# Routing of an expert-choice layer on one core: two token chunks sorted at once, a threshold from two lists, 512-column output products, and dummy products on TensorE

## The chip, the cores and the metric

The kernel runs on 1 core of one Trainium2 chip. The metric is the device time of one execution in microseconds (us), given as the median of several runs. About 0.3% (3 us) is what a measurement of this kernel can tell from no change.

## What is computed

One encoder layer on 512 tokens of width 1024: three token mixers (neighbourhood attention, grouped-query attention, cross-attention into 256 memory tokens), each gated and projected, and then the part in which the change lies:

```
mix    = merged @ w_out
x      = layer_norm(alpha * x + mix)
logits = x @ w_router                      # 512 tokens x 16 experts
aff    = softmax(logits, axis=experts)
gate, idx = top_k(aff.T, 64)               # each expert takes its 64 best tokens
xs     = x[idx]
h      = xs @ w_gate_up[e];  ye = (silu(hg) * hu) @ w_down[e] * gate
x      = layer_norm(alpha * x + scatter_add(ye))
```

All inputs are float32. The weights of the 16 experts are 192 MB (12 MB each), the rest of the weights about 37 MB.

## The kernel before, in words

Everything is in one function with a schedule written out by hand: each engine (TensorE, VectorE, ScalarE, GpSimd) and each DMA queue works through its instructions strictly in program order, and a tile that is used again waits for its last reader. Tokens lie in four chunks `m` = 0 to 3 of 128.

**Weights of the mixers.** They come as 74 units of 128 x 1024 (512 KB), loaded by the SP queue two ahead into two "raw" tiles. ScalarE casts each to a high part (L84) and VectorE subtracts to get a low part (L85); a product is then three products, high x high, high x low and low x high, in a fast float32 format. The last 8 units are `w_out`. A unit's parts sit in rotating tiles, so unit i can be split only when unit i-3 is used up.

**Output products (L964 to L985 and `w_half`, L991).** `merged` lies transposed in `mh` and `ml` (high and low part). For the first 512 columns, two passes of 256 columns run over all four chunks; each pass takes two units (one for each half of the 1024-long inner dimension), and its four accumulators lie in the PSUM tags S, S, T, T for the first pass and mm, mm, mm, Y for the second. Then the other 512 columns are done chunk by chunk in halves of 256 columns (`w_half`, with 24 products each). `wo_evac` (L910) adds alpha x to each accumulator and takes statistics of 256 columns at a time on VectorE.

**Routing of a chunk.** `r_transpose` (L892) transposes the unnormed sum on TensorE and ScalarE copies it; `r_logits` (L901) multiplies it with the router's weights (which already hold the norm's gain, centred), in two halves that VectorE adds. `route` (L916) works out the row scale 1/sqrt(var) by three Newton steps on 128 x 1 columns, scales the logits, and makes the softmax (exponential on ScalarE). `r_back` (L946) transposes the 128 x 16 result to 16 x 128, and ScalarE copies it into `affA` or `affB`. `x1_norm` (L953) makes the normed rows: two small GpSimd steps, a scale and a cast of 128 x 1024 on ScalarE (L957, L959), and a subtraction on GpSimd (L960); the gather needs these.

**The sort (`rounds`, L996).** Each expert's threshold is its 64th best value. One round finds the 8 best of a row (MAX8) and replaces them by -1 (MATCH_REPLACE8); eight rounds give 64. A chunk's 64 best are put beside the next chunk and both are sorted again: chunk 0 (128 columns), chunk 1 with the best of 0, and, behind everything (L1069), chunks 2 and 3 with the best so far (264 to 320 columns). The sorts of chunks 0 and 1 are mixed with the steps of `route`. 16 partitions (one per expert) are in use. The steps of `w_half` and of routing follow each other as L1014 to L1064 have them.

**Threshold and gather.** The 64th value of each expert (L1071) is spread to all partitions by a product (`thp`, L1073), VectorE compares, `cnp` counts places by products with a triangle matrix (`tri_t`), `onehot` (L1095) builds 0/1 matrices and `gather` (L1105) picks the rows by products: 8 pieces for each group of four experts. For the first expert three pieces are made, and then pieces and gate/up products (`gate_up`, L1140, the products of L1149) alternate.

**Expert weights (`Ring`, L715).** They are loaded as 192 MB in pieces of 1 MB into 20 places that other tiles leave free, in a fixed order, issued by the SP queue. Places 7 to 10 (raw tiles among them) come free while w_out is split; 11 to 16 hold `mh`, the last split unit, `ml` and the low parts until the output products are done; 17 and 18 hold x until `x1_norm` is done; 19 holds the triangle matrix until the counts are done. Loads 20 and on wait until `gate_up` has used up a place (`done`, L770).

Of the kernel before, what the change touches and what calls it, by code (L numbers as in the profile page):

```python
# [40 lines left out]
def layer_kernel(ctx: ExitStack, tc: tile.TileContext, xt, xn, memt, wu, bgate, rpb, gains, wrt,  # L41
# [838 lines left out]
    def x1(m):  # L880
        return X1[m // 2][:, m % 2]
# [5 lines left out]
    affA = R("t", [NEXP, P + 192], "affA", bufs=2)  # L887
    affB = R("t", [NEXP, 320], "affB", bufs=2)

    XT, LG, MV, RS = {}, {}, {}, {}  # L890

    def r_transpose(m, k0, n, eng="act"):  # L892
# [6 lines left out]
        (nc.scalar.copy if eng == "act" else nc.vector.tensor_copy)(t, tp)  # L899

    def r_logits(m, h):  # L901
        lg = PB("mm", f"lg{m}{h}")
        for k in range(4 * h, 4 * h + 4):
            nc.tensor.matmul(lg[:, :NEXP], XT.pop((m, k)), wg_t[:, k], start=(k == 4 * h), stop=(k == 4 * h + 3))
        if h:
            LG[m] = lg
        else:
            nc.scalar.copy(lgA[:, m], lg[:, :NEXP])

    def wo_evac(m, acc, c0, n):  # L910
        c = slice(c0, c0 + n)
        nc.vector.scalar_tensor_tensor(x1(m)[:, c], x1(m)[:, c], DN_ALPHA, acc[:, :n], op0=ALU.mult, op1=ALU.add)
        for q in range(c0 // 256, (c0 + n) // 256):
            nc.vector.bn_stats(st_all[:, m, q], x1(m)[:, q * 256:(q + 1) * 256])

    def route(m):  # L916
        mv = small([P, 2], "lnmv")
        MV[m] = mv
        nc.vector.bn_aggr(mv, st_all[:, m])
        yield  # L920
        v, hv, y, a = (small([P, 1], n) for n in ("rv_v", "rv_h", "rv_y", "rv_a"))
        nc.vector.tensor_scalar(v, mv[:, 1:2], LN_EPS, None, op0=ALU.add)
        yield
        nc.vector.tensor_scalar(y.bitcast(I32), v.bitcast(I32), -0.5, RSQRT_SEED, op0=ALU.mult, op1=ALU.add)
        nc.vector.tensor_scalar(hv, v, -0.5, None, op0=ALU.mult)
        yield
        for i in range(3):
            nc.vector.tensor_scalar(a, y, hv, y, op0=ALU.mult, op1=ALU.mult)
            if i == 2:
                nc.vector.tensor_tensor(lgA[:, m], lgA[:, m], LG.pop(m)[:, :NEXP], op=ALU.add)  # L930
            yield
            nc.vector.tensor_scalar(y, a, 1.5, y, op0=ALU.add, op1=ALU.mult)
            yield
        RS[m] = y
        nc.vector.scalar_tensor_tensor(lgA[:, m], lgA[:, m], y, rb, op0=ALU.mult, op1=ALU.add)
        yield
        nm, sm, rc = (small([P, 1], n) for n in ("rnm", "rsm", "rrc"))
        nc.vector.tensor_reduce(nm, lgA[:, m], axis=AX.X, op=ALU.max, negate=True)
        ex = small([P, NEXP], "rex")
        nc.scalar.activation(ex, lgA[:, m], AF.Exp, bias=nm, accum_out=sm)  # L940
        yield
        nc.vector.reciprocal(rc, sm)
        yield
        nc.vector.tensor_scalar(aff[:, m], ex, rc, None, op0=ALU.mult)

    def r_back(m):  # L946
        ap = PB("Y", f"ap{m}")
        nc.tensor.transpose(ap[:NEXP, :P], aff[:, m], ident)
        c = (0, P + 64, 64, 64 + P)[m]
        dst = (affA if m < 2 else affB)[:, c:c + P]  # L950
        nc.scalar.copy(dst, ap[:NEXP, :P])

    def x1_norm(m):  # L953
        nb, r = (small([P, 1], n) for n in ("lnnb", "lnr13"))
        nc.gpsimd.tensor_scalar(r, RS[m], X_SCALE, None, op0=ALU.mult)
        nc.gpsimd.tensor_scalar(nb, MV[m][:, 0:1], r, -1.0, op0=ALU.mult, op1=ALU.mult)
        nc.scalar.activation(x1(m), x1(m), AF.Identity, bias=nb, scale=r)  # L957
# [6 lines left out]
    for q in range(2):  # L964
        banks = ("mm", "mm", "mm", "Y") if q == 1 else ("S", "S", "T", "T")
        accs = [PB(banks[m], f"wo{q}{m}") for m in range(NT)]
        for hf in range(2):
            u, = ws.take()
            h = u[0].rearrange("p (k c) -> p k c", k=4)
            lo = u[1].rearrange("p (k c) -> p k c", k=4)  # L970
            ws.prefetch(2)
            for m in range(NT):
                tok = slice(m * P, (m + 1) * P)
                acc = accs[m][:, :256]
                for k in range(4):
                    kk = 4 * hf + k
                    nc.tensor.matmul(acc, mh[:, kk, tok], h[:, k], start=(kk == 0), stop=False)
                    nc.tensor.matmul(acc, mh[:, kk, tok], lo[:, k], start=False, stop=False)
                    nc.tensor.matmul(acc, ml[:, kk, tok], h[:, k], start=False, stop=(kk == KD - 1))  # L979
                if hf == 1:  # L980
                    wo_evac(m, accs[m], q * 256, 256)
                    if q == 1 and m:
                        r_transpose(m - 1, 0, 4)
                    if q == 1 and m > 1:
                        r_logits(m - 2, 0)  # L985
    us = [ws.take(2)]
    ws.prefetch(2)
    us.append(ws.take(2))
    ring.upto(N_EARLY + 2)

    def w_half(m, j, hooks={}):  # L991
        acc = PB("S", f"woc{m}{j}")
        n_chunk(acc[:, :256], us[j], mh, ml, m, hooks)
        wo_evac(m, acc, 512 + j * 256, 256)

    def rounds(src, lead, dst):  # L996
        for r in range(8):
            win = src[:, lead - 8 * (r + 1) if lead else 0:]
            t = dst[:, 56 - 8 * r:64 - 8 * r]
# [14 lines left out]
    w_half(0, 0)  # L1014
    r_transpose(3, 0, 4)
    r_logits(2, 0)
    w_half(0, 1)
    r_logits(3, 0)
    r_transpose(0, 4, 2)
    w_half(1, 0)  # L1020
    r_transpose(0, 6, 2)
    r_logits(0, 1)
    all_of(route(0))
    w_half(1, 1)
    r_transpose(1, 4, 2)
    r_back(0)
    x1_norm(0)
    seg = rounds(affA[:, 0:P], 0, affA[:, P:P + 64])
    c1 = route(1)
    for _ in range(5):  # L1030
        steps(c1, seg)
    w_half(2, 0, {2: lambda: r_transpose(1, 6, 2)})
    r_logits(1, 1)
    for _ in range(8):
        steps(c1, seg)
    all_of(c1)
    all_of(seg)
    w_half(2, 1)
    r_transpose(2, 4, 2)
    r_back(1)  # L1040
    x1_norm(1)
    seg = rounds(affA[:, P:], 64, affB[:, 0:64])
    c2 = route(2)
    for _ in range(5):
        steps(c2, seg)
    w_half(3, 0, {2: lambda: r_transpose(2, 6, 2)})
    r_logits(2, 1)
    for _ in range(8):
        steps(c2, seg)
    all_of(c2)  # L1050
    x1_norm(2)
    w_half(3, 1)
    r_transpose(3, 4, 2)
    r_transpose(3, 6, 2)
    r_back(2)
    r_logits(3, 1)
    c3 = route(3)
    for _ in range(8):
        steps(c3, seg)
    all_of(c3)  # L1060
    all_of(seg)
    r_back(3)
    x1_norm(3)
    ring.upto(len(RING))  # L1064
# [3 lines left out]
    top = cp.tile([NEXP, 64], F32, name="top")  # L1068
    all_of(rounds(affB, 64, top))  # L1069
# [521 lines left out]
```

## Time and profile before

| | us |
|---|---|
| runs shown | 998.05, 998.72, 1001.01 |
| median | 998.72 |
| the profiled execution | 997.83 |
| its span, first to last instruction | 995.9 |
| TensorE busy | 955.8 (96%) |
| VectorE busy | 459.5 (46%) |
| ScalarE busy | 273.8 (27%) |
| GpSimd busy | 75.2 (8%) |
| mean granted clock of TensorE | 0.988 |

A profile line by group reads: source line, engine, operation, written tile, read tiles, shapes, count, then busy time, mean duration of one in ns, and the idle time of the engine ahead of it with what ended it. A line in order of time reads: start, duration, engine, line, operation, shapes, count, and in brackets the idle time ahead. SPq is the SP engine's DMA queue. A line of the table by stretch reads: from:to, length, busy time (and count) of PE, PEld (weight loads of TensorE), DVE, ACT and POOL, then the granted clock, the DMA engines' share and their GB/s. A busy TensorE is not one at its peak, since ends of products are modelled. TensorE's products of float32 are recorded as two.

### The profile page before, as it was taken

The numbers are of one execution on the slowest core, as the hardware profiler recorded it, in microseconds if no ns is written. First come the engines' busy times: TensorE is split into PE (matmuls) and PEld (weight loads), VectorE is DVE, ScalarE is ACT, GpSimd is POOL, SyncE is SP. The second block draws the span as 40 slices with busy tenths as digits, with TensorE's granted clock in tenths as the row PEclk, the third lists the DMA queues.
The fourth block names the chain that finished last, engine by engine and source line by source line (L and its number), as shares of the span: only waits on it lengthen the run. The fifth ranks groups of instructions, "written<-read, shape, count | busy, mean of one in ns | idle before, by whom it ended". The sixth has DMA issues, their size and how long they took to land.

```text
span 995.9 us, 13692 instructions
## 1 busy us (share of the span) xinstructions
PE 955.8 (96%) x5504; PEld 631.3 (63%) x5504; DVE 459.5 (46%) x897; ACT 273.8 (27%) x547; POOL 75.2 (8%) x77
## 2 busy tenths in 40 slices
PE   7999899999999999999968999999999999998998
PEld 7899787889888888889954334533353333432355
DVE  5437678664376566256582155331322222231327
ACT  5434345444354444333341010200020001100021
POOL 0002403000131231000040000000000000000002
PEclk9999999999999999999987999999999999999999
DMA  8221211111432332665448999999999999999992
GB/s 340 98 85 65 64 64 43 64 48 61 110 113 81 93 88 94 237 253 222 159 180 339 368 424 420 423 421 422 425 423 422 424 424 424 423 422 421 425 397 97
DMA packets 67422, 251.61 MB, mean 253 GB/s; under 512 B 14720, under 2 KB 19488, under 8 KB 54944
## 3 DMA queue, kind: packets, MB, share of 16 engines
q1 hardware_dynamic: 66784, 249.44, 64.1%
q10 hardware_dynamic: 576, 1.31, 0.3%
q8 instruction: 43, 0.70, 0.3%
q14 instruction: 19, 0.16, 0.0%
HBM read 247.84 MB, written 2.10 MB: 251 GB/s over the span
## 4 chain that ended last, share of the span: by engine, by line
PE 80%; DMA 9%; DVE 6%; ACT 2%; POOL 2%; issue 1%; SPq 0%; POOLq 0%; ACTq 0%
PE g L1149 10%; PE u L1149 9%; PE y L1182 8%; DMA gu<-in_wgu 5%; PE gate L231 4%; PE gate L233 4%; PE gate L232 4%; DMA dn<-in_wdn 3%; PE pr L231 2%; PE ga L1113 2%; PE pr L232 2%; PE pr L233 2%; PE cb L1249 2%; PE ga L1115 2%; PE nqk L233 1%; PE nqk L232 1%
## 5 line engine op out<-in xcount | busy, mean ns | idle before, releaser
L1149 PE MATMUL g<-gu,xs 128*64 128x512 f32 x512 | 134.6, 604 | 5.5 <-DMA gu<-in_wgu 5.4
L85 DVE TENSOR_TENSOR wlo<-raw,whi 128x1024 fp32r<-128x1024 f32 (+2 forms) x75 | 92.7, 1237 | 87.7 <-ACT whi L84 87.3
L1149 PE MATMUL u<-gu,xs 128*64 128x512 f32 x512 | 131.6, 592 | 0.2 <-DMA gu<-in_wgu 0.2
L1182 PE MATMUL y<-dn,hT 128*64 128x512 f32 x480 | 106.8, 594 | 2.4 <-DMA dn<-in_wdn 2.2
L84 ACT CAST yh<-y 64x512 fp32r<-64x512 f32 x30 | 17.4, 579 | 249.0 <-PE y L1182 221.1
L84 ACT CAST whi<-raw 128x1024 fp32r<-128x1024 f32 (+2 forms) x75 | 77.0, 1027 | 25.3 <-PE wo L979 9.4
L1149 PEld LDWEIGHTS u<-gu,xs 128*64 128x64 f32 x512 | 36.7, 137 | 73.6 <-issue 68.3
L85 DVE TENSOR_TENSOR yl<-y,yh 64x512 fp32r<-64x512 f32 x30 | 20.7, 689 | 135.7 <-ACT yh L84 125.1
L1182 PEld LDWEIGHTS y<-dn,hT 128*64 128x64 f32 x480 | 33.8, 137 | 72.1 <-issue 63.1
L1149 PEld LDWEIGHTS g<-gu,xs 128*64 128x64 f32 x512 | 31.3, 136 | 62.4 <-issue 43.9
L1252 DVE TENSOR_TENSOR acc<-acc,cb 128x512 f32<-128x512 f32 x56 | 35.4, 683 | 35.1 <-PE cb L1250 35.1
L1170 DVE COPY hT<-ht 128x512 f32<-128x512 f32 x16 | 11.0, 690 | 62.1 <-PE ht L1167 62.1
L1314 POOL TENSOR_TENSOR acc<-acc,ln2g 128x512 f32<-128x512 f32 x4 | 5.1, 1277 | 452.3 <-DVE l2s L1326 452.1
L231 PE MATMUL gate<-xha,whi 128*128 128x512 f32 x96 | 38.9, 406 | 0.0
L232 PE MATMUL gate<-xla,whi 128*128 128x512 f32 x96 | 37.5, 390 | 0.0
L233 PE MATMUL gate<-xha,wlo 128*128 128x512 f32 x96 | 37.5, 390 | 0.0
L233 PE MATMUL gate<-xhb,wlo 128*128 128x512 f32 x96 | 37.4, 389 | 0.0
L231 PE MATMUL gate<-xhb,whi 128*128 128x512 f32 x96 | 37.3, 389 | 0.0
L232 PE MATMUL gate<-xlb,whi 128*128 128x512 f32 x96 | 37.3, 389 | 0.0
L550 ACT ACTIVATE gp<-gs,nm 128x512 f32<-128x512 f32 x32 | 21.7, 683 | 52.3 <-DVE nm L549 52.3
L1159 ACT ACTIVATE tg<-g 128x512 f32<-128x512 f32 x16 | 9.6, 597 | 89.5 <-PE g L1149 89.5
L1160 DVE SCALAR_TENSOR_TENSOR tg<-tg,g 128x512 f32<-128x512 f32 x16 | 11.0, 685 | 38.7 <-ACT tg L1159 38.7
(382 smaller groups left out, 1990.3 us busy)
## 6 DMA issues: line engine op xcount, KB each, us to landing
gu<-in_wgu SPq DMA_DIRECT2D x95, 1024.0 KB
dn<-in_wdn SPq DMA_DIRECT2D x49, 1024.0 KB
raw<-in_wu SPq DMA_DIRECT2D x73, 512.0 KB
gu<-in_wgu SPq DMA_DIRECT2D x66, 512.0 KB
dn<-in_wdn SPq DMA_DIRECT2D x30, 512.0 KB
xr<-in_xt SPq DMA_DIRECT2D x4, 512.0 KB
x<-in_xn SPq DMA_DIRECT2D x2, 1024.0 KB
bf<-in_rpb SPq DMA_DIRECT2D x64, 24.0 KB
```

The source lines that it names most:

```text
L84: nc.scalar.copy(hi, src)
L85: nc.vector.tensor_tensor(lo, src, hi.bitcast(F32), op=ALU.subtract)
L231: nc.tensor.matmul(acc, w_h, rh[:, k], start=(k == 0), stop=False)
L232: nc.tensor.matmul(acc, w_h, rl[:, k], start=False, stop=False)
L233: nc.tensor.matmul(acc, w_l, rh[:, k], start=False, stop=(k == nk - 1))
L550: nc.scalar.activation(self.p[:, h], self.s[h], AF.Exp, bias=nm[:, h:h + 1], accum_out=self.sm[:, h:h + 1])
L1113: nc.tensor.matmul(g, XH[m // 2][:, m % 2, c], oh[:, m], start=(m == 0), stop=False)
L1115: nc.tensor.matmul(g, XL[:, m, c], o16[:, m], start=False, stop=(m == NT - 1))
L1149: nc.tensor.matmul(GU[e][b][hf * 64:hf * 64 + 64], xs, w[b][:, hf * 512:hf * 512 + 512], start=(k == 0), stop=(k == KD - 1))
L1182: nc.tensor.matmul(y[o * 64:o * 64 + 64], hT[:, c, hf * 64:hf * 64 + 64], w[j][:, o * 512:(o + 1) * 512], start=(k == 0 and j == 0), stop= ...
L1249: nc.tensor.matmul(cb, g[:, m], yh[:, c], start=True, stop=False)
L1252: nc.vector.tensor_tensor(a, a, cb, op=ALU.add)
```

## The change

- **Units of w_out** hold 256 rows and 512 columns instead of 512 rows and 256 columns. The first 512 columns are one pass of 512-column products, with accumulators in mm, mm, mm, Y. Of the rest, chunks 0 to 2 are done with 512 columns at once and chunk 3 in two halves of 256; statistics are taken over 512 or 256 columns.
- **Transposes and logits** are hooked between the products, four blocks at a time; the second half of the logits starts with a product of the identity and the first half, in place of VectorE's addition.
- **Row scales** of chunks 0 and 1 are worked out together (128 x 2), then those of 2, then of 3; so are softmaxes.
- **Sorting:** chunks 0 and 1 go to partitions 0 to 15 and 32 to 47 of one tile `a01` and are sorted at once (48 partitions, 128 columns); their 64 best go ahead of chunks 2 and 3 in `a23`, in the same partitions, which are sorted at once behind everything (136 to 192 columns).
- **Threshold:** each expert then has two descending lists of 64. ScalarE copies the second one reversed, VectorE takes the maximum of the two place by place and the minimum over the places.
- **Norms:** `x1_norm` of chunks 2 and 3 stands behind the last transposed copy (`r_back(3)`), that of 1 behind a transposed copy of chunk 3; the small columns come from `norm_cols`.
- **Dummy products** (`keep_warm`, 128 x 128 with the identity, into a bank that nothing reads): 9 ahead of the last row scale, 26 behind the last transpose, 3 behind the counts.

```diff
+    def r_logits(m, k0, n=4):
+        if k0 in (0, 4):
+            LG[m] = PB("mm", f"lg{m}{k0}")
+        lg = LG[m][:, :NEXP]
+        if k0 == 4:
+            nc.tensor.matmul(lg, ident, lgA[:, m], start=True, stop=False)
+        for k in range(k0, k0 + n):
+            nc.tensor.matmul(lg, XT.pop((m, k)), wg_t[:, k], start=(k == 0), stop=(k in (3, 7)))
+        if k0 == 0:
+            nc.scalar.copy(lgA[:, m], lg)
...
+    accs = [PB(("mm", "mm", "mm", "Y")[m], f"wo{m}") for m in range(NT)]
+    for kp in range(4):
+        u, = ws.take()
+        ws.prefetch(2)
+        for m in range(NT):
+            wo_part(accs[m], m, u, kp, 0, 512, kp == 3)
+            if kp == 3:
+                wo_evac(m, accs[m], 0, 512, 0)
+                if m:
+                    r_transpose(m - 1, 0)
+                if m > 1:
+                    r_logits(m - 2, 0)
...
+    def w_rest(m, c, n, q, hooks={}):
+        acc = PB("S", f"woc{m}{c}")
+        for kp in range(4):
+            hooks.get(kp, lambda: None)()
+            wo_part(acc[:, :n], m, us[kp], kp, c, n, kp == 3)
+        wo_evac(m, acc, 512 + c, n, q)
...
+    warm2 = PB("T", "warm2")
+    def keep_warm(n):
+        for _ in range(n):
+            nc.tensor.matmul(warm2[:, :P], ident, ident, start=True, stop=True)
...
+    w_rest(0, 0, 512, 1, {1: lambda: r_transpose(3, 0), 2: lambda: r_logits(2, 0), 3: lambda: r_logits(3, 0)})
+    w_rest(1, 0, 512, 1, {1: lambda: r_transpose(0, 4), 3: lambda: r_logits(0, 4)})
+    all_of(row_scale((0, 1), 2))
+    norm_cols((0, 1))
+    w_rest(2, 0, 512, 1, {1: lambda: r_transpose(1, 4), 2: lambda: r_logits(1, 4),
+                          3: lambda: all_of(affinity((0, 1)))})
+    s2 = row_scale((2,), 2)
+    seg = rounds(a01, 0, a23[:, 0:64], True)
+    def sort_first():
+        for _ in range(8):
+            steps(s2, seg)
+    w_rest(3, 0, 256, 1, {0: lambda: r_back(0), 1: then(lambda: r_back(1), sort_first), 2: lambda: r_transpose(2, 4),
+                          3: lambda: r_logits(2, 4)})
+    all_of(s2)
     x1_norm(0)
+    norm_cols((2,))
+    f2 = affinity((2,))
+    def third():
+        x1_norm(1)
+        steps(f2)
+        all_of(seg)
+        all_of(f2)
+    w_rest(3, 256, 256, 2, {1: then(lambda: r_transpose(3, 4, 2), third), 2: lambda: r_logits(3, 4, 2)})
     r_transpose(3, 6, 2)
     r_back(2)
+    r_logits(3, 6, 2)
+    keep_warm(9)
+    all_of(row_scale((3,), 3))
+    norm_cols((3,))
+    all_of(affinity((3,)))
     r_back(3)
+    x1_norm(2)
     x1_norm(3)
+    keep_warm(26)
     ring.upto(len(RING))
...
-    all_of(rounds(affB, 64, top))
+    all_of(rounds(a23, 64, top, False))
+    rev = cp.tile([NEXP, 64], F32, name="rev")
+    nc.scalar.copy(rev, top[32:48, ::-1])
+    nc.vector.scalar_tensor_tensor(rev, rev, 1.0, top[:NEXP], op0=ALU.mult, op1=ALU.max)
+    cut = small([NEXP, 1], "cut", bufs=1)
+    nc.vector.tensor_reduce(cut, rev, axis=AX.X, op=ALU.min)
...
+    keep_warm(3)
     nc.vector.tensor_tensor(cnt, cnp, msk, op=ALU.mult)
...
-    units += [nu(w_out, q * 256, h) for q in range(4) for h in range(2)]
+    units += [wide(w_out, o * 512, kp) for o in range(2) for kp in range(4)]
```

`wo_part` makes the three products for two of the eight 128-row blocks of a unit; `row_scale` and `affinity` hold the steps of the old `route`.

More of the change, by code (lines that the diff above doesn't have):

```diff
@@ L986, in layer_kernel, with wo_part @@
-    us = [ws.take(2)]
+    def wo_part(acc, m, u, kp, c, n, last):
+        h, lo = (x.rearrange("p (k c) -> p k c", k=2) for x in u)
+        tok = slice(m * P, (m + 1) * P)
+        for k in range(2):
+            kk = 2 * kp + k
+            nc.tensor.matmul(acc, mh[:, kk, tok], h[:, k, c:c + n], start=(kk == 0), stop=False)
+            nc.tensor.matmul(acc, mh[:, kk, tok], lo[:, k, c:c + n], start=False, stop=False)
+            nc.tensor.matmul(acc, ml[:, kk, tok], h[:, k, c:c + n], start=False, stop=(kk == KD - 1))
@@ L1034, in layer_kernel, with then @@
[L1034 to L1053, printed above, removed]
+    def then(*fs):
+        return lambda: [f() for f in fs]
```

159 lines of the change are left out of this document (58 added, 101 removed).

## The prediction

> **What bounds the kernel now.** I read the page first (clock by slices), then the chain of waits, then tables by stretch, then instructions in order of time.
>
> ```profile
> span 995.9 us, 13692 instructions
> PEclk9999999999999999999987999999999999999999
> ```
> ```profile
> 946.51 16.01 DMA dn<-in_wdn
> 962.57 1.94 PE y L1182 x8
> ```
> ```profile
> 509.57:534.60 25.03, 11.75 (x87) 9.58 (x87) 16.41 (x65) 8.08 (x17) 5.73 (x6) 0.59 0.96 375
> 534.60:538.50 3.90, 3.90 (x22) 1.67 (x24) 0.55 (x1) 0.56 (x1) 0.00 (x0) 1.00 0.34 74
> 538.50:558.00 19.50, 18.64 (x100) 8.02 (x98) 3.72 (x13) 1.87 (x4) 0.00 (x0) 1.00 0.92 334
> 558.00:962.50 404.50, 393.84 (x1916) 156.59 (x1912) 117.47 (x202) 44.66 (x81) 0.00 (x0) 1.00 1.02 422
> ```
>
> The only dip of the clock lies in slices 21 and 22 (498 to 548 us): the routing stage. In the chain the last weights are waited for until 962.5; 33.4 us of last products, norm and stores follow, which the change doesn't touch. In the table by stretch (last three columns: clock, DMA share, GB/s) the stream of expert weights is full from 558 to 962.5 us. A full stream can't be shortened, so **the end is the moment at which the stream becomes full, plus fixed work.** Before that it loses 3.2 us in 534.6 to 538.5 (0.29 MB moved of 1.65) and 4.1 us in 538.5 to 558 (19.5 x (1 - 334/422)).
>
> ```profile
> 509.57 0.33 SPq L756 DMA_DIRECT2D gu<-in_wgu  x1
> 511.01 1.93 SPq L756 DMA_DIRECT2D dn<-in_wdn  x4
> 536.47 9.29 SPq L756 DMA_DIRECT2D gu<-in_wgu  x4
> ```
>
> Why it loses them: the ring of weight tiles has 20 places. Places 11 to 16 are loaded when the w_out products let go of their left operands (issues at 509.57 and from 511.01), 17 to 19 after the norms and the counts; these nine loads of 2.48 us (1.05 MB at 422 GB/s) end at 534.6. Load 20 is issued at 536.47, when the first gate/up products (G, 534.50 below) have released a place, and up to 558 the releases, not the stream, set the pace. So an earlier G moves the end one for one, up to the 7.3 us that are lost between, plus what the loads 11 to 16 gain themselves.
>
> **The path to G.**
>
> ```profile
> 454.18 0.28 PE L977 MATMUL wo<-whi,mha 128*128 128x256 f32 x1
> 455.62 0.28 PE L977 MATMUL wo<-whi,mha 128*128 128x256 f32 x1
> 510.81 0.29 PE L248 MATMUL woc<-wlast,mlb 128*128 128x256 f32 x1
> 517.78 0.42 DVE L1000 MAX8 top<-affB 16x8 f32<-16x264 f32 x1 [0.84 <-ACT affB L951]
> 525.48 0.22 DVE L1071 TENSOR_SCALAR dg<-ident,top 16x16 f32<-16x16 f32 x1
> 528.91 1.65 PE L1113 MATMUL ga<-oh,xA 128*128 128x256 f32 x4 [1.10 <-DVE oh L1100]
> 531.09 1.20 PE L1113 MATMUL ga<-oh,xA 128*128 128x256 f32 x4
> 534.50 1.08 PE L1149 MATMUL g<-gu,xs 128*64 128x512 f32 x4
> ```
>
> Products until 511.1; 6.7 us for the last chunk's norm, softmax and copies; 7.7 us of last sort; 3.4 us of threshold, counts, one-hot; 5.6 us for three of eight gathers. The change goes along this path.
>
> **(1) 512-column products.** Twelve products lie between the first two rows above: 0.12 us for 256 columns. For 512 columns 24 lie between these two:
>
> ```profile
> 437.64 0.39 PE L233 MATMUL pr<-ynh,wlo 128*128 128x512 f32 x1
> 443.08 0.39 PE L233 MATMUL pr<-ynh,wlo 128*128 128x512 f32 x1
> 457.05 0.69 DVE L861 SCALAR_TENSOR_TENSOR tm<-sg,pr 128x512 f32<-128x512 f32 x1
> ```
>
> 0.2267 us. So 384 x 0.12 = 46.1 us becomes 168 x 0.2267 + 48 x 0.12 = 43.8: 2.2 us less. Against it, the four second logits groups start with a product by the identity, in place of VectorE's addition: two short records each, 0.8 us at the most by the 0.1 us of a 128-column record. And the first accumulators now lie in the three "mm" banks, in which the projections before them end. The last is read by VectorE until 457.74, while TensorE comes to its third accumulator at 454.18 + 12 x 0.2267 = 456.9: 0.9 us of new stall. That leaves 0.5 us; of the old order's own stalls (56.9 us, of which products 46.1 and about 8.9 of transposes, logits and copies back) I let 0.7 of 1.9 us go. The products end at about 509.9, 1.2 us earlier, and with them loads 11 to 16. Bounds 0 to 2.5 us.
>
> **(2) To the last sort; norms.** VectorE now has the first sort between chunk 2's scale steps and ahead of the last evacuation, which also stands behind chunk 2's exponential, and that behind chunk 1's norm on ScalarE:
>
> ```profile
> 517.66 1.24 ACT L957 ACTIVATE x<-x,lnnb,lnr 128x1024 f32<-128x1024 f32 x1
> 518.93 1.04 ACT L959 CAST xA<-x 128x1024 fp32r<-128x1024 f32 x1
> 520.05 2.34 POOL L960 TENSOR_TENSOR xlo<-x,xA 128x1024 f16<-128x1024 f32 x1 [3.78 <-ACT xA L959]
> ```
>
> Chunk 0's norm (2.3 us) ends at about 506.6 and chunk 1's, behind one transposed copy, at 509.8; the exponential, reciprocal and scale follow until 510.9, so the last evacuation waits 0.9 us (its price to G is the same). Queued behind it on VectorE are the last statistics, scale and sort, for which everything waits. Behind it no other sort steps are mixed in any more: 5.2 us instead of 6.1 from evacuation to sorted row. The sort begins at about 516.1, **1.7 us earlier**; bounds -1 (another 2.3 us norm in front) to 2.5. Norms 2 and 3 move behind the last copy: the sort covers their 4.6 us on ScalarE, and GpSimd's lower parts end at 523, before the gather needs them (527) and before the ring needs their tiles (528).
>
> **(3) The sort.** Two chunks lie in 48 partitions, 136 to 192 columns a step, where one list had 264 to 320.
>
> ```profile
> L1000 DVE MAX8 top<-affB 16x8 f32<-16x264 f32 (+7 forms) x8 | 3.6, 453 | 1.1 <-ACT affB L951 0.8
> L1003 DVE MATCH_REPLACE8 affB<-top,affB 16x264 f32<-16x264 f32 (+6 forms) x7 | 3.0, 430 | 0.0
> 502.42 0.28 DVE L1000 MAX8 affA<-affA 16x8 f32<-16x128 f32 x1
> ```
> ```profile
> L85 DVE TENSOR_TENSOR yl<-y,yh 64x512 fp32r<-64x512 f32 x30 | 20.7, 689 | 135.7 <-ACT yh L84 125.1
> L1252 DVE TENSOR_TENSOR acc<-acc,cb 128x512 f32<-128x512 f32 x56 | 35.4, 683 | 35.1 <-PE cb L1250 35.1
> ```
>
> From 128 columns (0.28) to 264 (0.42) a column costs 1.05 ns; 64 and 128 partitions cost the same in the last two rows, so I price 48 as 16. Fifteen steps, each 128 columns narrower: 15 x 128 x 1.05 ns = 2.0 us; with the gaps rounded, **1.7 us less**. Bounds 0 (partitions cost) to 2.0.
>
> **(4) Threshold.** New on the path: ScalarE's reversed copy, a maximum, a minimum, each some 0.2 us plus the hand-over, by the 0.22 of the dg row: **0.75 us more**; bounds 0.5 to 1.2.
>
> Sum so far, with the clock as before: 1.7 + 1.7 - 0.75 = 2.6 us.
>
> **(5) The dummies and the clock.**
>
> ```profile
> 510.18:513.59 3.41, 1.83 (x15) 1.30 (x13) 3.10 (x17) 3.04 (x7) 0.63 (x2) 1.00 0.86 291
> 513.59:517.01 3.42, 1.65 (x8) 1.53 (x8) 2.45 (x13) 0.62 (x4) 2.49 (x3) 0.50 0.93 305
> 527.24:530.65 3.41, 2.31 (x28) 1.86 (x25) 1.95 (x6) 1.41 (x4) 0.00 (x0) 0.50 1.03 435
> 530.65:534.07 3.42, 3.42 (x18) 2.85 (x17) 0.55 (x1) 0.56 (x1) 0.00 (x0) 0.50 0.99 410
> ```
> ```profile
> 526.40 0.22 DVE L1076 TENSOR_TENSOR msk<-rt,thp 128x64 f16<-128x64 f32 x1 [0.70 <-PE thp L1073]
> 527.85 0.29 DVE L1085 TENSOR_TENSOR rt<-cnp,msk 128x128 f32<-128x128 f32 x1 [1.09 <-PE cnp L1084]
> 536.36 0.74 PE L1113 MATMUL ga<-oh,xA 128*128 128x256 f32 x4
> 537.48 1.08 PE L1149 MATMUL g<-gu,xs 128*64 128x512 f32 x4
> 980.07 4.18 PE L1348 MATMUL warm_l<-ident 128*128 128x128 f32 x36
> ```
>
> The clock fell to 0.50 after 3.4 us with TensorE busy 54% (first row) and came back after 3.4 us of 100% (fourth), not of 68% (third). At 0.50 a gather took 1.7 us ((534.50 - 531.09) / 2), at 1.0 1.12 us (536.36 to 537.48). A held clock is thus worth 2 x 0.6 us in gathers two and three, about 0.6 in the first and 0.6 in threshold and counts (the two waits, 0.70 and 1.09, by a third): 2.4 us. A dummy has two records of 4.18/36 = 0.116 us: the 9 take 2.1 us, the 26 take 6.0 (515.4 to 521.4, under the sort, which ends at 522.1), the 3 take 0.7. The dg product comes at 523.2. So TensorE is idle 521.4 to 523.2 and half idle until the gather at 525.7: 3.4 us around there have about 35 to 50% of work, under the 54% that lost the clock before. I expect it to fall between 523.4 and 526.4 and to come back 3.4 us later, in the second or third gather. Of the 2.4 us I take 1.4; bounds 0 and 2.4, and below (a late rival) less than nothing.
>
> [...]
>
> **Sum: 2.6 + 1.4 = 4.0 us.** The profiled execution took 997.83 us (span 995.9 and 1.9 around it), which gives 993.8. The median of the runs shown lies 0.9 higher, which would give 994.7; I forecast **994.2**, between the two, and the rivals below are set against the same base. Load 19 would then end at 533.5 (1.1 us earlier) and load 20 be released at 532.5: the stream has no gap left there, and the slow stretch after it moves with G.
>
> **Rivals.** (A) *The clock is held throughout*: 5.0 us, 993.2. For it: no idle stretch of TensorE is longer than 1.8 us. Against: the 54% row, whose longest idle time was about 1 us. [...]
> (B) *The clock is lost until G*, as before: 2.6 us, 995.6. For it: 68% did not bring it back.
> (C) *The dummies themselves delay the sort and the threshold.* At half clock 9 take 4.2 us and push the last transpose from 515.3 to 516.9, 26 take 12.1 us, to 529.1, and the dg product, queued behind them, comes at 529.1 instead of 525.76: 3.4 us later than now, 1001.6. It decides when the clock stays at 0.50 for more than some 3 us of the 26. Against: dense work brought it back within 3.4 us (fourth row).
> (D) *The stream hides G*: if what the stream loses until 558 is its own doing and not the releases', only the 1.1 us of loads 11 to 16 remain: 997. Against: load 20's issue follows G by 2.0 us.
> (E) *VectorE becomes the bound*: the first sort or the norm ahead of chunk 2's exponential costs 2 us more than in (2): 996.2. The same if the 512-column products bring nothing. For it: by my times VectorE is behind TensorE from 501 on.
>
> **How the numbers follow.** Forecast 0.45 (993 to 995.4), A 0.17, B 0.14, C 0.05, D 0.09, E 0.10. The measurement can tell 0.3%, 3.0 us, from no change: faster below 995.7. Faster: 0.44 of the forecast, A, and a fifth of B: 0.64. Slower: C and a remainder: 0.06. Same: 0.30. The range goes from A less 1.7 us for the bounds of (1) and (2), 991.5, to D with the spread of the runs, 998.0; C lies outside.
>
> **What would show it.** Products ending at 509 to 510.5; the wait for the projection's evacuation in the third accumulator (0.9 us); the last sort starting near 516 and lasting 6.0; MAX8 over 48 partitions at 0.28 to 0.36; a clock of 0.5 that covers less than two gathers; G near 530.5; no gap of the stream between loads 19 and 20; and every later row shifted by G's gain. A G that is earlier by more than the end is would prove the step from G to the end wrong; so would dummy records 0.23 us apart for the whole of the sort.

## The result and the profile after

The changed kernel takes 1003.26 us (median of 20 runs, 1000.15 to 1005.35) where the kernel before, beside it on the same chip, takes 998.04 (20 runs): a ratio of 1.0039 (95% interval 1.0029 to 1.0049). 994.2 was predicted. It is slower by about the least that can be told from no change. The profiled execution took 1000.53 us, one of the shorter of the 20. So the trace below accounts for 2.7 us over the trace before (997.83), while the medians lie 5.2 us apart; what the longer executions do besides, this trace doesn't show.

The page of the changed kernel, span and clock by slices; then its table by stretch, same columns as before:

```profile
span 998.5 us, 13482 instructions
PEclk8999999999999999999988999999999999999999
```
```profile
509.57:534.60 25.03, 19.42 (x145) 17.62 (x145) 16.78 (x59) 8.95 (x18) 8.51 (x8) 0.79 0.96 352
534.60:538.50 3.90, 3.90 (x18) 2.26 (x18) 0.54 (x1) 0.56 (x1) 0.00 (x0) 0.60 0.46 174
538.50:558.00 19.50, 18.64 (x102) 8.42 (x100) 2.57 (x11) 1.84 (x4) 0.00 (x0) 1.00 0.85 309
558.00:962.50 404.50, 394.07 (x1918) 156.56 (x1914) 117.94 (x202) 45.25 (x82) 0.00 (x0) 1.00 1.02 420
```

The routing stretch now runs at a mean clock of 0.79 instead of 0.59, and still the full stream begins later. The path to the first gate/up product, in order of time:

```profile
510.86 0.28 PE L990 MATMUL woc<-wlast,mlb 128*128 128x256 f32 x1
520.54 0.29 DVE L1021 MAX8 top<-a 48x8 f32<-48x136 f32 x1 [2.52 <-ACT a L964]
527.95 0.22 DVE L1093 SCALAR_TENSOR_TENSOR dg<-ident,cut,rt 16x16 f32<-16x16 f32 x1
531.11 1.65 PE L1136 MATMUL ga<-oh,xA 128*128 128x256 f32 x4 [0.33 <-DVE oh L1123]
535.02 1.20 PE L1136 MATMUL ga<-oh,xA 128*128 128x256 f32 x4
537.03 1.40 PE L1172 MATMUL g<-gu,xs 128*64 128x512 f32 x4
```

The products end where they did (511.14, before 511.10). The last sort starts 2.76 us later (before 517.78), the diagonal is 2.47 later, the first gate/up product 2.53 later. The chain's end has `965.28 1.94 PE y L1205 x8`, before 962.57: 2.71 later. The loss is made between 511 and 520.5 us, and hardly anything after it changes the sum.

What happens there, VectorE, GpSimd and TensorE in order of time:

```profile
511.48 1.92 DVE L957 SCALAR_TENSOR_TENSOR rt<-r_ex,r_rc,rt 128x16 f32<-128x16 f32 x1
513.32 0.41 DVE L920 SCALAR_TENSOR_TENSOR x<-x,woc 128x256 f32<-128x256 f32 x1
```
```profile
511.03 2.34 POOL L978 TENSOR_TENSOR xlo<-x,xA 128x1024 f16<-128x1024 f32 x1 [0.35 <-ACT xA L977]
```
```profile
513.78 0.69 PE L903 MATMUL x1t<-ident,x 128*128 128x128 f32 x2 [2.65 <-DVE x L920]
515.81 4.19 PE L1042 MATMUL warm<-ident 128*128 128x128 f32 x18
519.79 0.42 PE L962 MATMUL ap<-ident,rt 128*16 128x128 f32 x1
520.01 6.28 PE L1042 MATMUL warm<-ident 128*128 128x128 f32 x52
```

Chunk 2's scale step, 128 x 16 elements, takes 1.92 us; the same step takes 0.24 for chunk 3 (at 517.78). It ends at 513.40, GpSimd's subtraction of chunk 1 at 513.37. The last evacuation stands behind it, so TensorE has nothing for 2.65 us. Then the clock falls (columns: TensorE's busy time first, the clock third from the end):

```profile
513.00:514.00 1.00, 0.21 (x1) 0.22 (x2) 0.97 (x3) 0.00 (x0) 0.37 (x1) 0.91 0.97 311
514.00:515.00 1.00, 0.75 (x4) 0.26 (x3) 0.86 (x6) 0.49 (x2) 0.00 (x0) 0.50 1.04 397
519.00:520.00 1.00, 1.00 (x6) 0.92 (x6) 0.00 (x0) 0.00 (x0) 0.00 (x0) 0.50 1.01 410
521.00:522.00 1.00, 1.00 (x12) 1.00 (x11) 0.90 (x5) 0.97 (x2) 0.00 (x0) 1.00 1.03 422
```

Before that fall TensorE was busy for 0.76 of 3.41 us (510.41 to 513.82). At 0.50 the 9 dummies need 4.19 us instead of 2.1, and the last transpose, ready with chunk 3's scale at 518.02, waits behind them until 519.79: 1.8 us. The same pair of engines meets again behind the sort:

```profile
526.58 1.10 DVE L1089 SCALAR_TENSOR_TENSOR rev<-rev,top 16x64 f32<-16x64 f32 x1 [0.31 <-ACT rev L1088]
```
```profile
522.93 4.67 POOL L978 TENSOR_TENSOR xlo<-x,xA 128x1024 f16<-128x1024 f32 x2 [5.69 <-ACT xA L977]
```

The maximum of the two lists takes 1.10 us and ends at 527.68, 0.08 after GpSimd's two subtractions.

### The profile page after: what moved, and what is told of

Read it like the earlier page. It is cut to its first block, busy times and chain, and to the rows that moved or that the text cites. A ratio compares the mean times of both kernels' runs of the same rounds, so it can differ in the third digit from the quotient of the medians.

```text
span 998.5 us, 13482 instructions
## 1 busy us (share of the span) xinstructions
PE 966.9 (97%) x5420; PEld 634.1 (64%) x5420; DVE 454.0 (45%) x851; ACT 273.8 (27%) x545; POOL 75.1 (8%) x78
## 4 chain that ended last, share of the span: by engine, by line
PE 76%; DMA 12%; DVE 6%; ACT 2%; POOL 2%; issue 1%; SPq 0%; POOLq 0%; DVEq 0%; ACTq 0%
PE g L1172 9%; PE u L1172 8%; PE y L1205 8%; DMA gu<-in_wgu 6%; DMA dn<-in_wdn 5%; PE gate L231 4%; PE gate L232 4%; PE gate L233 4%; PE ga L1136 2%; PE ga L1138 2%; PE nqk L231 1%; PE nqk L232 1%; PE nqk L233 1%; PE gy L574 1%; PE pr L231 1%
## 5 line engine op out<-in xcount | busy, mean ns | idle before, releaser
L1205 PE MATMUL y<-dn,hT 128*64 128x512 f32 x480 | 106.8, 594 | 2.4 <-DMA dn<-in_wdn 2.2
L1205 PEld LDWEIGHTS y<-dn,hT 128*64 128x64 f32 x480 | 33.8, 137 | 72.1 <-issue 63.4
L550 ACT ACTIVATE gp<-gs,nm 128x512 f32<-128x512 f32 x32 | 21.7, 683 | 52.3 <-DVE nm L549 52.3
```

Source lines behind the costliest of these rows:

```text
L550: nc.scalar.activation(self.p[:, h], self.s[h], AF.Exp, bias=nm[:, h:h + 1], accum_out=self.sm[:, h:h + 1])
L1205: nc.tensor.matmul(y[o * 64:o * 64 + 64], hT[:, c, hf * 64:hf * 64 + 64], w[j][:, o * 512:(o + 1) * 512], start=(k == 0 and j == 0), stop= ...
```

## The experiments

Theories on record: **P**, VectorE stands still while GpSimd's subtraction runs, in steps that have two tensors in SBUF (the memory of the tiles; PSUM holds TensorE's products); **K**, the dummies stand in TensorE's queue and cost double at half clock (4.19 us for the 9 at 0.50, where 2.1 was reckoned); **S**, the steps are slow by their own form. The routing stage starts at times that differ by up to 1.9 us from execution to execution (the products end at 510.9 to 512.8 us), so places below are counted from the products' end, as each trace has it. "thp" is the threshold product, "y end" the end of the last full down product; "late spell" is a stretch at half clock between 945 and 957 us, told of at the end.

| kernel | last sort | thp | first gate/up | y end behind it | late spell | median | ratio to before |
|---|---|---|---|---|---|---|---|
| before | 6.7 | 14.7 | 23.4 | 430.0 | 0 | | |
| after | 9.4 | 17.1 | 25.9 | 430.2 | 0 | 1003.26 | 1.0039 [1.0029, 1.0049] |
| e1_port | 5.9 | 12.8 | 19.5 | 430.6 | 0 | 997.31 | 0.9984 [0.9968, 1.0000] |
| e2_nodummy | 7.7 | 15.4 | 24.4 | 429.8 | 0 | 999.44 | 1.0009 [0.9994, 1.0024] |
| e3_port_nodummy | 6.0 | 12.9 | 21.6 | 431.7 | 3.4 | 998.07 | 0.9989 [0.9972, 1.0006] |
| e4_before_dummies | 7.6 | 15.6 | 22.4 | 433.0 | 6.8 | 1000.05 | 1.0005 [0.9990, 1.0020] |
| e5_pool_later | 7.0 | 14.7 | 21.7 | 433.2 | 6.8 | 999.17 | 0.9999 [0.9983, 1.0014] |
| e6_without_nine | 7.7 | 15.4 | 22.0 | 434.3 | 6.8 | 1000.19 | 1.0010 [0.9996, 1.0024] |
| e7_more_dummies | 5.9 | 12.8 | 19.3 | 431.2 | 3.4 | 996.09 | 0.9965 [0.9949, 0.9981] |
| e8_banks | 6.0 | 12.8 | 19.8 | 431.6 | 0 | 997.17 | 0.9980 [0.9966, 0.9995] |
| e9_best | 6.1 | 13.4 | 19.9 | 430.0 | 0 | 994.84 | 0.9962 [0.9946, 0.9978] |
| e10_rows_apart | 8.3 | 16.0 | 23.2 | 429.7 | 0 | 1000.27 | 1.0018 [1.0002, 1.0034] |
| e11_scale_only | 6.6 | 14.4 | 21.7 | 433.2 | 6.8 | 999.52 | 1.0000 [0.9985, 1.0015] |
| e12_one_input | 8.3 | 16.0 | 23.1 | 430.4 | 0 | 1002.20 | 1.0027 [1.0012, 1.0041] |

**Both conflicts taken away, dummies kept.** The exponential goes to PSUM, the reversed list too, and ScalarE makes the diagonal.

```diff
-            nc.scalar.activation(ex[:, m], lgA[:, m], AF.Exp, ...)
+            nc.scalar.activation(EX[m], lgA[:, m], AF.Exp, ...)      # EX[m] = LG[m][:, NEXP:2 * NEXP]
-    nc.scalar.copy(rev, top[32:48, ::-1])
+    nc.scalar.copy(rev_p, top[32:48, ::-1])                          # rev_p in PSUM
-    nc.vector.scalar_tensor_tensor(dg, ident[:NEXP, :NEXP], cut, ...)
+    nc.scalar.activation(dg, ident[:NEXP, :NEXP], AF.Copy, scale=cut)
```

> The changed kernel, but the three VectorE steps with two operands in SBUF lose one of them: the exponential and the reversed list are written to PSUM, and the 16 x 16 diagonal is made on ScalarE. Theory P (a VectorE step with two SBUF operands stands still while GpSimd's 2.4 us lower-part subtraction runs): the 1.92 us scale of chunk 2 falls to about 0.25 and the 1.10 us maximum to about 0.25, the wait of TensorE for the last evacuation falls by 1.7 us, and the time falls by at least 2.6 us, by 4 if the clock then stays up for the 9 dummies. Rival K (the dummies on TensorE's queue at half clock are the loss): the two steps may shrink, but the median stays within 1.5 us of the changed kernel's 1003.3. Rival S (these steps are slow by their form or shape): they stay long.

Its trace, VectorE, GpSimd, TensorE:

```profile
512.19 0.23 DVE L957 SCALAR_TENSOR_TENSOR rt<-lg,r_rc,rt 128x16 f32<-128x16 f32 x1
517.78 0.29 DVE L1021 MAX8 top<-a 48x8 f32<-48x136 f32 x1 [0.74 <-ACT a L964]
523.77 0.21 DVE L1090 SCALAR_TENSOR_TENSOR rev<-rev_p,top 16x64 f32<-16x64 f32 x1 [0.27 <-ACT rev_p L1089]
```
```profile
511.74 2.35 POOL L978 TENSOR_TENSOR xlo<-x,xA 128x1024 f16<-128x1024 f32 x1 [0.34 <-ACT xA L977]
520.17 4.67 POOL L978 TENSOR_TENSOR xlo<-x,xA 128x1024 f16<-128x1024 f32 x2 [3.90 <-ACT xA L977]
```
```profile
512.80 0.44 PE L902 MATMUL x1t<-ident,x 128*128 128x128 f32 x2 [0.96 <-DVE x L919]
514.17 2.25 PE L1042 MATMUL warm<-ident 128*128 128x128 f32 x18
531.35 1.08 PE L1173 MATMUL g<-gu,xs 128*64 128x512 f32 x4
```

GpSimd runs beside both steps as in the changed kernel, and they take 0.23 and 0.21 us, now that one input comes from PSUM. TensorE idles 0.96 instead of 2.65, the clock holds, the 9 dummies take 2.25, and the last sort starts 3.5 us sooner than in the changed kernel: 1.7 of it the stall, 1.8 the dummies. The ratio falls from 1.0039 to 0.9984, by some 5.5 us, more than K alone allowed (1.5); against the kernel before, 0.9984 is hardly to be told from no change.

**Dummies taken away**, alone and together with the conflicts (every `keep_warm` of the stage removed).

> The changed kernel without any dummy product. Theory K: the median falls from 1003.3 to about 999 to 1000 and the spread of 5 us between executions goes, since the last transpose no longer waits for 9 dummies at half clock (1.75 us in the profile) nor the threshold product for 26. Theory P alone: the two long VectorE steps stay (1.9 and 1.1 us), the time falls by less than 2 us, and the spread stays.

> Both edits. If P and K each hold, the last sort starts at about 517 and the first gate/up product comes near 532.5: 995.5 to 996.5, faster than before by about 2 us. If only one holds, the time is that of the run with the one edit.

e2's median is 999.44, as K had it, but its executions still spread over 5 us (998.20 to 1003.20), which K had not. e3's first gate/up product came 21.6 us behind the products, near the 21.4 expected, but the median is 998.07 instead of 995.5 to 996.5; its trace has a late spell.

The four cases from the table, first gate/up product behind the products' end: with conflicts 25.9 (dummies) and 24.4 (none); without conflicts 19.5 and 21.6. In these traces the dummies cost 1.5 us where VectorE is held and are worth 2.1 where it is not. One trace is one draw, though: two more with the held step and the dummies (e10, e12) have 23.2 and 23.1. The ratios say that with the conflicts the dummies cost 3 us (1.0039 against 1.0009, intervals apart), and without them no difference can be told (0.9984 against 0.9989). So the price of the dummies hangs on the conflicts; a gain from them isn't shown by these four.

**The dummies alone in the kernel before** (9, 26 and 3 at the same places).

> The kernel before with the same 9, 26 and 3 dummies at the corresponding places and nothing else. Theory K: the clock has fallen when the 9 begin, so they take about 4 us instead of 2 and push the last transpose by some 2 us: 1000 to 1001 with a wider spread. Theory P: no change, 998. The prediction's own step (5): the clock is held for part of the gather, 996.5 to 997.5.

The last sort starts 0.9 us later than before (the 9 take 3.55 us, partly at half clock), the first gate/up product 1.0 earlier, and the ratio of 1.0005 shows no gain: the median of 1000.05 is K's number (1000 to 1001), not the 996.5 to 997.5 of the prediction's step (5). The wider spread that K had with it did not come.

**GpSimd moved instead of the operands:** chunk 1's norm behind the last transposed copy of chunk 3.

```diff
     def third():
-        x1_norm(1)
...
     r_transpose(3, 6, 2)
+    x1_norm(1)
```

> The changed kernel with chunk 1's norm (ScalarE 2.3 us, then GpSimd's subtraction 2.34 us) moved from ahead of chunk 2's exponential to behind the copy of chunk 3's last two transposes. Every VectorE instruction keeps its form. Theory P (a VectorE step that reads both tensors from SBUF stands still while GpSimd's subtraction runs): chunk 2's scale step, 1.92 us in the changed kernel, takes 0.24; TensorE idles 1.0 us instead of 2.65 behind the products; the subtraction now runs about 4.1 to 6.5 us after the products' end and meets chunk 3's scale step there, which grows from 0.24 to 1 or 1.5 us and ends with the subtraction; the maximum of the threshold stays at 1.1. First gate/up product 21 to 24 us after the products' end instead of 25.9; median 999 to 1001.5. Rival S (these steps are slow by their form or by what stands before them): chunk 2's step stays at 1.9 us, chunk 3's at 0.24, and the median stays at 1003.

```profile
511.41 0.23 DVE L957 SCALAR_TENSOR_TENSOR rt<-r_ex,r_rc,rt 128x16 f32<-128x16 f32 x1
516.03 1.52 DVE L957 SCALAR_TENSOR_TENSOR rt<-r_ex,r_rc,rt 128x16 f32<-128x16 f32 x1
```
```profile
515.18 2.34 POOL L978 TENSOR_TENSOR xlo<-x,xA 128x1024 f16<-128x1024 f32 x1 [4.36 <-ACT xA L977]
```

With every VectorE instruction as it was, the stall has moved from chunk 2 to chunk 3 and ends at 517.55 with the subtraction (517.52). S falls; P is shown in its main point, the stall goes where GpSimd goes. The first gate/up product (21.7) and the median (999.17) lie where P had them.

**Only the scale step freed; and freed by another form.** In e11 the exponential is in PSUM but the reversed list stays in SBUF. In e12 nothing is in PSUM, but the step is the kernel before's, one tensor times one scalar:

```diff
-            nc.vector.scalar_tensor_tensor(aff[:, m], ex[:, m], rce[:, m:m + 1], ones_f[:, :NEXP], op0=ALU.mult, op1=ALU.mult)
+            nc.vector.tensor_scalar(aff[:, m], ex[:, m], rce[:, m:m + 1], None, op0=ALU.mult)
```

> The changed kernel with the exponential in PSUM and the diagonal on ScalarE, but the reversed list in SBUF as in the changed kernel: only the first of the two conflicts is taken away. Theory P: chunk 2's scale step 0.23 us, the last sort starts 5.9 us after the products' end (9.4 in the changed kernel), and the maximum is now held until GpSimd's two subtractions end, 13.0 us after the products' end (0.9 us longer than 0.21); threshold product 13.7 us after, where the kernel without both conflicts has 12.8; first gate/up product about 20.4 after; median 998.2. Rival S for the second place (the maximum is slow only because it follows ScalarE's copy of the list): it takes 0.21 here, threshold product 12.8, median 997.3.

> The changed kernel with the scale step of the softmax written as the kernel before has it: the exponential times one scalar for each partition, without the second tensor of ones; the exponential stays in SBUF. Nothing else differs. Theory P2 (what GpSimd's subtraction holds up is a VectorE step with two tensors in SBUF, not any step that reads SBUF): chunk 2's step takes 0.21 to 0.24 us although the subtraction runs beside it, TensorE idles 1.0 us behind the products instead of 2.65, the last sort starts 6 to 6.6 us after the products' end (9.4), the maximum of the threshold is held as before (1.1 us), and the median is 999 to 1000. Rival P1 (any VectorE step reading SBUF is held): the step stays at 1.9 us and the median at 1002 to 1003.

The maximum of e11, then GpSimd; the scale step of e12, then GpSimd:

```profile
524.50 1.11 DVE L1089 SCALAR_TENSOR_TENSOR rev<-rev,top 16x64 f32<-16x64 f32 x1 [0.31 <-ACT rev L1088]
```
```profile
520.86 4.68 POOL L978 TENSOR_TENSOR xlo<-x,xA 128x1024 f16<-128x1024 f32 x2 [4.58 <-ACT xA L977]
```
```profile
512.89 1.92 DVE L957 TENSOR_SCALAR rt<-r_ex,r_rc 128x16 f32<-128x16 f32 x1
```
```profile
512.44 2.34 POOL L978 TENSOR_TENSOR xlo<-x,xA 128x1024 f16<-128x1024 f32 x1 [0.34 <-ACT xA L977]
```

e11: the maximum is held until 525.61, the subtractions' end is 525.54, as expected. Not as expected, the last sort came at 6.6 and not 5.9: the clock fell at 514.7 although nothing stalled, and the 9 dummies took 3.75 us; the median is 999.52, 998.2 was expected. So the 9 dummies can delay the transpose even without the conflict.

e12: my narrower theory (two tensors in SBUF) falls. The step with one SBUF tensor is held for the same 1.92 us; the new form of the step is not the cause, only the place. The median stayed at 1002.20, as the rival P1 had it. Nor is every step that reads SBUF held. In the changed kernel the sort and the 128 x 1 steps run beside a subtraction at their normal 0.27 and 0.20 us:

```profile
508.20 0.20 DVE L938 TENSOR_SCALAR r_y<-r_a,r_y 128x1 f32<-128x1 f32 x1
509.88 0.27 DVE L1024 MATCH_REPLACE8 a<-a,a 48x128 f32<-48x128 f32 x1
```
```profile
507.74 2.39 POOL L978 TENSOR_TENSOR xlo<-x,xA 128x1024 f16<-128x1024 f32 x1 [7.34 <-ACT xA L977]
```

What separates the held 128 x 16 step from these no run here settles. What was measured is where the stalls end: within 0.1 us of the subtractions' ends (513.40 and 513.37, 527.68 and 527.60 in the changed kernel; 517.55 and 517.52 in e5; 525.61 and 525.54 in e11; 514.81 and 514.78 in e12). Why they end there, and why the form with one tensor is held like that with two, isn't shown.

**The 9 alone taken away.**

> The changed kernel without the 9 dummies; the 26 and the 3 stay. Theory K (dummies stand in TensorE's queue, twice as long at half clock, and the clock comes back only at the end of a 3.4 us window that was busy throughout): the last transpose goes right behind chunk 3's scale step, the last sort starts 1.75 us sooner (7.6 us after the products' end instead of 9.4), but all 26 dummies start at half clock, take 8 to 10 us instead of 6.3 and end after the cut diagonal is there, so that the threshold product waits up to 2 us; first gate/up product 24 to 26 us after the products' end; median 1001 to 1003.5, most of the gain given back. Rival (only the 9 do harm): the whole 1.75 us comes back, first gate/up product 24 us after, median 1001 or less, threshold product not waiting for dummies.

The last transpose went right behind the scale step (last sort 7.7 us after the products instead of 9.4), and the 26 dummies, starting at half clock, took 7.71 us; the diagonal came after them, so that the threshold product waited for nothing. The rival held: the first gate/up product came at 22.0, and in this trace the 26 do no harm, the 9 do.

**More dummies; other accumulators.** 32 and 5 for 26 and 3; and, in e8, the first pass in banks S, S, mm, Y.

> The kernel without the two conflicts of VectorE with GpSimd (exponential and reversed list in PSUM, diagonal on ScalarE), with 32 dummies instead of 26 under the last sort and 5 instead of 3 behind the counts, so that TensorE has no idle time above 0.5 us between the last transpose and the gather. Theory K: with every window busy the clock stays at 1.0 until the gate/up products; three gathers take 0.92 us each, the first gate/up product comes 18 us after the products' end instead of 19.5; median 996. Rival: the clock falls all the same (the counts and the threshold are too thin), the dummies take twice as long and the first gate/up product comes 20 us or more after the products' end; median 998 to 999.

> The kernel without the two conflicts, with the first pass of w_out accumulating in banks S, S, mm, Y instead of mm, mm, mm, Y. If the wait of the third accumulator for VectorE's reading of the projection before (0.45 us, and 0.5 us of longer products around it) is what ate the gain of the 512-column products, the stage from the first w_out product to the last takes 56.0 us instead of 57.0, and the median falls by 1 us to 996.3. Rival (the stage is paced by its evacuations, copies and logits): the wait moves to a later place, 57.0 us remain, 997.3.

e7: the clock stayed at 1.00 from the products to the experts, but the first gate/up product came at 19.3 and not 18: the first gather's high products took 1.39 us at full clock (0.72 in the next gather), with their one-hot matrices only just made. e8: the stage of products took 56.54 us instead of 56.98; 0.4 of the 1.0 expected, the rest came back as waits elsewhere, and the median of 997.17 is that of e1 (997.31).

**The narrow products apart.** In the last expert 16 products of 32 contraction rows (the norm's scale) and 16 more (its rows) stand one behind the other; the second 16 move behind one k of gate/up products. e9 has this and all that helped; e10 is the changed kernel with this alone.

```diff
-            all_of(rows_of_norm())
-            gate_up(e, range(4, KD))
+            gate_up(e, (4,))
+            all_of(rows_of_norm())
+            gate_up(e, range(5, KD))
```

> All that helped so far in one kernel: no conflicts of VectorE with GpSimd, 32 and 5 dummies, first pass of w_out in banks S, S, mm, Y, and the 16 products of the last norm's rows (32 contraction rows each) moved from right behind the 16 of its scale to behind one more k of the last expert's gate and up products. Theory L (the clock is lost in any window of 3.4 us with more than about 2.5 us of these narrow products, and where the windows fall is chance): no fall of the clock near 946 to 950 us, products stage 56.5 us, first gate/up product 19.3 us after the products' end, mean clock 0.996, median 994.5 to 995.5, below both kernels. Rival (the spell near 946 us has another cause or costs nothing, since the weights end last anyway): a spell of 3.4 us is still there, or the median stays at 996.

> The changed kernel with nothing but those 16 narrow products moved apart. Theory L: the changed kernel's typical execution (1003.3, mean clock 0.986) is 2.7 us longer than its profiled one (1000.5, clock 0.990) because it loses one or two windows of 3.4 us there; with the products apart its median falls to about 1001 and no execution lies under a mean clock of 0.987. Rival R: the difference comes from the routing stage, where the dummies run at half clock for one window more in some executions; the median stays at 1003 and the spread of the clocks too.

e7 first, where the clock is lost there, then e9:

```profile
946.00:948.00 2.00, 2.00 (x9) 0.77 (x9) 1.57 (x3) 0.86 (x2) 0.00 (x0) 0.52 1.01 414
948.00:950.00 2.00, 2.00 (x8) 0.56 (x6) 0.77 (x2) 0.00 (x0) 0.00 (x0) 0.62 1.04 422
```
```profile
945.00:947.00 2.00, 2.00 (x16) 0.91 (x13) 0.00 (x0) 0.00 (x0) 0.00 (x0) 1.00 1.03 422
947.00:949.00 2.00, 2.00 (x15) 0.97 (x14) 1.20 (x3) 1.15 (x2) 0.00 (x0) 1.00 1.03 422
```

In e9 the 9 and the 32 dummies were at half clock for one window (514 to 518) and the threshold product waited for the last of them, 0.6 us later than in e1. Still e9 takes 994.84 us, 0.9962 [0.9946, 0.9978] of before: better than both kernels (part of it is the narrow products, which the kernel before has together too). e10 has a ratio of 1.0018 where the changed kernel has 1.0039, but the intervals overlap, and 4 of its 12 executions still lie at a mean clock of 0.985 to 0.987, where none was expected. Its trace has no late spell, but neither has the changed kernel's. So it isn't shown how much of the changed kernel's spread comes from these products and how much from the routing stage.

## Why the prediction was wrong

- **Products end 1.2 us earlier (1):** 0.0. From the first `w_out` product to the last there were 56.92 us before and 57.03 after. From product to product 47.5 became 47.1 us, not 43.8: the first product behind each group of transposes or logits takes 0.09 us longer, and around the third accumulator (0.45 us of wait, row below) the pitch is 0.34 to 0.36 instead of 0.227. The transposes and logits, with the identity, took 9.9 us instead of 9.4. "I let 0.7 of 1.9 go" for the old order's stalls was a guess in the direction of the forecast.

```profile
457.72 0.50 PE L988 MATMUL wo<-whi,mha 128*128 128x512 f32 x1 [0.45 <-DVE tm L861]
```

- **Last sort at 516.1 (2): the step that failed.** It came at 520.54, 2.76 us later than before, where I had 1.7 earlier and 1 later as the bound. I had placed the norm of chunk 1 ahead of chunk 2's exponential and counted ScalarE's 2.3 us, but not what its GpSimd part does to VectorE beside it. Of the 4.4 us missed, 1.2 are step (1), 1.7 the held scale step and 1.8 the 9 dummies at half clock, less 0.3 that the rest came sooner: without the held step and the delay (e1) the sort starts 0.7 us sooner behind the products than before, where (2) had 0.5 of its own.
- **Sort of 6.0 us (3): right.** 5.72 (520.54 to 526.26), before 7.67; 48 partitions cost no more than 16: a MAX8 over 192 columns takes 0.35 us in both kernels.
- **Threshold 0.75 us (4): right as a chain, wrong beside GpSimd.** From the sort's end to the threshold product 1.97 us against 0.31, 1.66 more; in e1, with the maximum free, 1.12, which is 0.81 more.
- **Clock and dummies (5): the fall after little work right, the order wrong, the gain not there.** I let the clock fall at 523 to 526, behind the dummies; it fell at 513.8, ahead of them. In all five traces with the held step of chunk 2 (after, e2, e6, e10, e12) it fell there, with TensorE busy 22 to 34% of the 3.41 us before; of the six with the dummies and without that step it fell there in two (e9, e11, 61%). So the missed stall went with the loss in every trace, but a loss can come without it. The second fall, 2.7 us behind the threshold product, lies where I had the only one, but lasted 6.8 us (530.9 to 537.7) and not 3.4, and covered all three gathers. From the threshold product to the first gate/up product it took 8.80 us, before 8.74: nothing of the 1.4 us came.
- **The sum.** I had the first gate/up product at 530.5, it came at 537.03. The 6.5 us are 4.4 of (2) with (1), less 0.3 of (3), 0.9 of (4) and 1.5 of (5). The median lies 2.7 us above the profiled execution on top of that; a late spell would be of that size (last point), but no trace of this kernel has one, and the cause stays open.
- **Rival C** had half the answer: it pushed the last transpose by 1.6 us, 1.8 were measured. Its other half, 26 dummies at half clock ahead of the threshold, didn't come (6.28 us in the changed kernel, 7.71 in e6). I gave it 0.05 because dense work had brought the clock back within 3.4 us; that held for the 26, but the 9 were over before the clock came back.
- **Rival E** came near: VectorE lost 1.7 us ahead of the last evacuation where E had 2, and the 512-column products brought nothing. But E gave the norm's and the sort's own time as the reason, not GpSimd beside VectorE, and took the two as alternatives: 996.2.
- **The end moves with the first gate/up product: right, where no late spell lies between.** 2.53 us there, 2.71 at the last weights, 2.6 in the span; over seven such executions "y end" lies 429.7 to 430.6 us behind (e8: 431.6, with 3.3 us of waits for down weights from 534 to 965 us where the changed kernel has 2.2). With a spell it is 1.2 to 4.3 us more, which the prediction hadn't.

## What to carry to other kernels

Before a GpSimd step is moved, lay its whole span over VectorE's list and look for steps like those held here (128 x 16 and 16 x 64, all tensors in SBUF), then price each at the rest of GpSimd's instruction (1.92 us for 0.24 and 1.10 for 0.21 here); the sort's steps were not held (0.27 us beside a subtraction). Dummies belong behind the instruction that waits, not ahead of it: the last transpose waited 1.8 us behind them, since the 9 took 4.19 us at a clock of 0.50 (2.25 at 1.00, e1). A held engine and a lost clock made each other dearer here (the dummies cost 3 us with the conflicts, without them no difference can be told), so take experiments in pairs (both, either, none) before saying what an edit is worth, and by medians, since single traces of one stage lay up to 2.8 us apart.

## What the hardware showed beyond that

**The clock is lost and given back in whole windows.** In the 1-us tables the spells at half clock between the products and the experts last 3.4 (e1, e8, e9; one or two such in e4, e5, e10 to e12), 6.8 (after, twice; e6), 17.1 (e3) and 20.5 us (before, e2): 1, 2, 5 and 6 times 3.41. Worked out from the clock column of the same tables, all falls and returns of one trace between 15 and 957 us lie on one grid with a step of 3.413 us, to within 0.02 us, in each of the 14 traces: in e4 at 16.38, 514.72, 518.14, 528.38, 531.80, 948.22 and 955.04, which is 0, 146, 147, 150, 151, 273 and 275 steps on. A window below is one step of a trace's grid. Where the windows fall differs from execution to execution: in three traces with the scale step held for 1.92 us the clock falls 2.7 (after), 4.2 (e10) and 3.9 us (e12) behind the products' end, and they have the first gate/up product at 25.9 (after), 23.2 (e10) and 23.1 us (e12). After the fall TensorE was busy 3.16 of the next 3.41 us in the changed kernel and got the clock back only after one window more; in e10 and e12 that window was full, and the clock came back at its end. Over all 14 traces, between the products and the experts, windows at full clock in which TensorE was busy 17 to 62% were followed by the loss, but some from 57% on were not, and of the windows at half clock only those of 99% or more gave the clock back.

**A busy TensorE can lose its clock.** The late spell begins while TensorE is 100% busy, in 32-row products. e7:

```profile
942.66 2.05 PE L1241 MATMUL g<-lnr,ident 32*128 32x128 f32 x16
944.63 2.21 PE L1290 MATMUL gbr<-lnr,gb_sel 32*6 32x128 f32 x16
```

Its clock falls at about 946.1 (0.52 over the 2 us from 946 is 0.08 at full clock), so the window before began at 942.7 and held nothing else. In the kernel before they ran from 945.71 to 949.52; counted on from 513.59 in steps of 3.413 us, the windows end at 947.08 and 950.50, with 1.4 and 2.4 us of them, and the clock held. A spell of one window went with 1.2 to 1.7 us at the end, one of two with 3.0 to 4.3 (table, y end). Laid out the same way, the fullest window of each of the twelve traces in which the 32 products stand together held 2.7 to 3.4 us of them in the six that lost the clock there (e3, e4, e5, e6, e7, e11) and 2.0 to 2.6 us in the six that kept it. That narrow products count for less than full ones is my reading; it fits e9 and e10, where they stand apart, no window held more than 2.1 us, and no spell came.
